# A decoder layer on one core: the last two pairs of the down projection interleaved, their joining done through accumulating transfers, and the final norm written into the plan

## The chip, the cores and the metric

One Trainium2 chip, one core. The metric is the device time of one launch in microseconds. Engines are named as in the profile: PE (TensorE matmul) and PEld (its weight loads), DVE (VectorE), ACT (ScalarE), POOL (GpSimd), SP (SyncE, which here only issues transfers).

## The reference, cut to what matters

One layer of a hybrid decoder for 512 prompt rows and 8 sample rows. Attention, gated linear attention and the projections before them are not touched. What matters is the end of the layer and the final norm:

```python
h = x + mix @ w_o
f = jnp.square(jax.nn.relu(rmsnorm(h, g_norm2) @ w_up))
x = h + f @ w_down            # D_MODEL = 1024, D_FF = 4096
...
y_prompt = rmsnorm(xp, g_final)
y_sample = rmsnorm(xs, g_final)
```

## The kernel before

All rows stand together as 520 columns, 1024 features as 8 tiles (k = 0 to 7) of 128 partitions. The columns are cut into two halves of 260: `one` and `two`. Products are float32 in three passes: a weight is split into a high part (`h`, on ACT) and the rest (`l`, on DVE), and every 128x128 tile is multiplied as high x high, high x low, low x high.

`w_up` and `w_down` are done in 32 *pairs* (units 0 to 31), in four rounds `qd`: four up pairs, then four down pairs for k = 0, 2, 4, 6. A pair makes two feature tiles in both column halves with seven products instead of eight (P1 to P7, each 4x3 = 12 matmuls), from sums and differences of the weights and columns. A unit has three banks in PSUM: `e` takes P5 and then P3, `a` takes P2 (added to a copy of P1, the job `ca`), `x` takes P1, P6, P7, P4 one upon another. The second column half of both tiles is complete after P7 (k5 and k6 save what the banks held in between; `f2` and `t2` add it). P2 and P4 only serve the first half.

The order of all instructions is written out in `PLAN`, one line for each unit. A token is a product (`P1`), a weight's job (`h7`, `l7`, and `s1 s2` for sums of weights) or a job of the unit, with `+` or `-` in front for the next or the previous unit. `pair_mm` goes through a line and issues each token; `turn` and `behind` hold ACT, DVE and PE to that order. DVE steps are issued at L165 (`add`) and L168 (`stt`), ACT steps at L162 (`act`), matmuls of pairs at L259, loads on SP at L121, the weight sums on POOL at L149.

The result `dd` collects the down pairs (`u1` to `u6`) over the first three rounds. In the last round, for tiles k and k+1: `r0 r1` (`settle`, L1488 for its transfer) multiply `dd` by `rv` (the norm's factor, squared, since relu squared is scaled by it afterwards) and add the residual `Hd` from DRAM with an accumulating transfer of POOL. `q` squares for the final norm (ACT), `w` adds the square to `tot` (DVE), `n` multiplies by the final norm's gain (ACT). For k = 4 the residual is not accumulated: `X` loads it with SP, `a0 a1` add it. For k = 6 the last partial sums are multiplied by `rv` before they are added: `m`, `y`, `q`, `w` with the letters `f` (tile 6, half two), `t` (tile 7, half two), `a` (tile 6, half one).

Behind the plan stands the end, in plain code from L1577 on: products of `tot` with ones for both halves (L1583); `rate` (Ln, a DVE step at L1593, Exp, square); the last quarter of `dd` (tile 7, half one) in two pieces of 130 columns, with its own product with ones; `root` (two DVE steps); and `put` (L1605, outputs at L1607), four pieces for half two and five for half one.

The last two lines of the plan before (units 30 and 31):

```
h7 -u5 l5 -r0 P1 h2 -u6 l6 l2 P5 ca l7 h4 -r1 --q1 P6 u1 --q0 l4 --n0 +s1 +h1 P3 u2 +s2 +l1 P7 +h6 --w1 -q0 u4 P2 u3 +h5 -w0 +l5 P4
h4 -u5 h3 l4 -r0 P1 h2 l6 -a0 P5 ca -u6 h7 l3 --n0 -r1 P6 k5 l2 --q1 l7 P3 k6 -a1 ---n1 --w1 -q0 P7 -q1 f2 -w0 --n1 mf P2 t2 yf mt qf -w1 P4 yt w0 qt nt w1 -n1 ma ya qa -n0 wa nf
```

Of the kernel before, what the change touches and what calls it, by code (L numbers as in the profile page):

```python
# [18 lines left out]
D = 1024  # L19
# [19 lines left out]
h7 l5 -x1 --u4 -u5 l6 P1 h2 l7 h3 l3 P5 ca -y0 +s1 P6 u1 -y1 h4 +h5 l4 P3 +X u2 +s2 -u6 l2 P7 +h6 x0 P2 u3 +h1 y0 +l1 P4
h7 l5 -x1 --u4 -y1 P1 l6 l7 P5 ca h3 h2 l3 P6 u1 +s1 h4 +s2 P3 u2 -u4 +h1 l2 l4 P7 +h6 +h3 P2 u3 +h5 +l6 -u6 x0 +l1 P4  # L40
h7 l5 -x1 l7 -u5 P1 -u4 -u6 -y0 h2 l3 --u5 P5 ca +s1 h4 -y1 P6 k5 l4 +h1 l2 +l1 P3 k6 +s2 P7 f2 +h6 +h3 P2 t2 +h5 +l3 rt2 rf2 +l6 P4
-sf2 l5 -st2 h7 -rf1 l7 P1 -ht2 h2 -c0 +s1 -sf1 -rt1 -c1 P5 ca -c3 -st1 +s2 -hT0 h4 l2 P6 k5 -lT0 +h1 -c2 -ht1 -lt2 -hT2 P3 k6 +l1 -hf1 -lT2 -hT1 -lt1 -lf1 P7 +h6 -lT1 l4 +h3 P2 t2 +h5 f2 rt2 +l5 st2 P4
-rf2 l3 -ht2 -sf2 l6 -rf1 -c0 -sf1 P1 +s1 h7 -c3 h2 l7 P5 ca +s2 -hf1 -rt1 l2 h4 P6 k5 -lt2 -c1 -st1 l4 -hT0 -hT1 -lT0 P3 k6 -c2 -ht1 -lf1 -hT2 -lt1 P7 f2 +h6 -lT2 +h1 -lT1 rf2 P2 t2 +h3 +l1 +h5 +l6 rt2 P4
-sf2 l3 -st2 -rf1 l5 h7 P1 -c0 -sf1 -rt1 +s1 -hf1 l7 h4 P5 ca l4 -st1 -ht2 -c1 -ht1 -c3 P6 k5 -lt1 -lt2 h2 -lf1 +h5 -c2 P3 k6 l2 -hT1 +s2 -hT2 -hT0 P7 -lT2 +h6 f2 -lT1 rf2 sf2 -lT0 P2 t2 +h1 +l5 rt2 st2 +l1 P4
-rf1 -sf1 -hf1 -c0 -c3 -lf1 P1 -hT0 -c1 -lT0 h3 -hT1 l6 P5 ca l3 -lT1 h2 h7 P6 u1 -ht2 -lt2 h4 l7 -rt1 P3 u2 -st1 +h1 -c2 l4 -hT2 -ht1 P7 l2 -lt1 -lT2 P2 u3 +s1 +l1 P4
h5 -u4 h6 l5 h7 s2 P1 l6 h3 l7 P5 ca -u5 h2 l3 h4 P6 u1 +h1 +s1 P3 u2 l4 l2 P7 +l1 u4 P2 u3 +h5 -u6 +h6 +s2 P4 Z
l6 h3 l5 h7 -u5 P1 l3 -u6 -z P5 ca +s1 h2 l7 h4 P6 u1 l4 l2 P3 u2 +s2 z0 P7 +h6 +h5 +l6 +h3 P2 u3 +h1 +l1 P4
h7 l5 -u4 -u5 P1 l3 l7 -z1 P5 ca h4 -u6 P6 u1 h2 +s1 +h1 P3 u2 l2 l4 P7 +s2 +l1 P2 u3 +h5 z0 +h6 +h3 P4
l6 l3 l5 P1 h7 -z1 h2 l7 P5 ca h4 l4 P6 k5 +s1 +h1 -u6 -u4 P3 k6 +s2 +l1 l2 P7 +h6 f2 +h3 +l6 rf2 P2 t2 +h5 rt2 +l5 sf2 P4
-st2 --u5 -rf1 l3 -ht2 -sf1 -c0 h7 P1 -c1 -rt1 -lt2 h2 -c3 +s1 P5 ca +s2 -hT0 -hT1 l2 P6 k5 l7 -st1 h4 -c2 -ht1 P3 k6 l4 -hT2 -lT1 +h1 -lT2 -hf1 P7 f2 +h6 -lT0 rf2 -lt1 +h3 -lf1 P2 t2 +h5 +l6 sf2 rt2 +l1 P4  # L50
-st2 l3 -rf1 -sf1 l5 -ht2 P1 h7 -c0 +s1 h2 -c3 -rt1 -c1 P5 ca l2 -st1 h4 l7 -ht1 P6 k5 l4 -hT1 +s2 -hT0 -lt2 -hf1 P3 k6 -lt1 -c2 +h1 -lT0 -lT1 P7 +h6 f2 -lf1 -hT2 +h3 -lT2 P2 t2 rf2 +h5 +l6 rt2 +l1 sf2 P4
h7 l5 -st2 l3 -rf1 -ht2 P1 -c0 -sf1 +s1 -rt1 -st1 -c3 -hf1 -c1 P5 ca l7 h4 +s2 h2 P6 k5 -lf1 l2 -hT1 -c2 -hT0 l4 -ht1 P3 k6 -lt2 +h5 -lT0 -hT2 -lt1 P7 f2 +h6 -lT2 rf2 -lT1 sf2 P2 t2 +h1 +l5 rt2 st2 +l1 P4
-rf1 -sf1 -hf1 l6 -c0 -lf1 h3 P1 -c3 -rt1 -hT0 -c1 -lT0 -hT1 P5 ca l3 -lT1 -st1 -ht1 P6 u1 h7 -ht2 l7 -lt2 h4 h2 P3 u2 -c2 l2 -hT2 +h1 P7 -lt1 l4 -lT2 P2 u3 +s1 +l1 +h6 P4
s2 h5 l5 P1 h7 h2 l7 l6 P5 ca h3 -u5 h4 l3 P6 u1 l2 P3 u2 +s1 l4 P7 +h6 +h1 P2 u3 +h7 -u6 +l1 P4
# [27 lines left out]
class Build:  # L82
# [155 lines left out]

    def pair_mm(self, plan):


        nc, i = self.nc, self.cur
        self.cur += 1
        acts, banks, jobs = self.units[i]
        self.load_sums(i)
        if i + 2 < len(self.panels):
            self.load_panel(i + 2)
        e = banks["e"] = self.pm.tile([P, 2, 512], F32, tag="m", name="mps")[:, 0, :HC]
        a, x = banks["a"], banks["x"] = [self.bank("mps")[:, :HC] for _ in range(2)]
        into = {"P5": e, "P3": e, "P2": a}  # L250
        for t in plan.split():
            n = t.lstrip("+-")
            if n[0] == "P":
                p, ks = n.split(".") if "." in n else (n, "0123")
                hi, lo = self.ready[i][p]
                for k in map(int, ks):
                    xh, xl = acts(p, k)
                    for y, (w, u) in enumerate(((hi, xh), (hi, xl), (lo, xh))):
                        mm = nc.tensor.matmul(into.get(p, x), w[:, k], u, start=(p in ("P1", "P5") and k == 0 and y == 0),  # L259
                                              stop=(k == 3 and y == 2), skip_group_check=True)  # L260
                        self.behind(mm, self.last)
                        self.last = mm
            else:
                j = i + t.count("+") - t.count("-")
                job = self.units[j][2] if j in self.units else {}
                job[n]() if n in job else self.weight(j, n)
# [963 lines left out]
    def run(self):  # L1230
# [159 lines left out]
        with pool("late") as p:  # L1390
# [70 lines left out]
            def extras(qd, k, b):  # L1461
# [23 lines left out]
                def settle(x):  # L1485
                    self.add(dd[:, k + x], dd[:, k + x], rv, op=ALU.mult)
                    if k != 4:
                        nc.gpsimd.dma_start(dd[:, k + x], Hd[:, k + x], accum_op=ALU.add)  # L1488
# [96 lines left out]
            def turn(m):  # L1585
                return self.turn("DVE", m)
# [195 lines left out]
```

## Time and profile before

| | |
|---|---|
| median of 3 runs | 872.91 us (872.46 to 873.63) |
| profiled execution | 870.76 us, of it the span 869.0 us |
| PE, DVE, ACT, POOL busy | 98%, 78%, 57%, 13% of the span |
| granted TensorE clock, mean | 0.994 |
| transfers | 187 MB, 216 GB/s in the mean |

Times in the profile count from the first instruction of the span. "Busy" is the union of an engine's instructions; matmuls are pipelined, so the recorded 0.28 us of one overlap, and a new one starts every 0.12 us. Idle time is shown with the engine that ended it.

### The profile page before, as it was taken

The numbers are of one execution on the slowest core, as the hardware profiler recorded it, in microseconds if no ns is written. First come the engines' busy times: TensorE is split into PE (matmuls) and PEld (weight loads), VectorE is DVE, ScalarE is ACT, GpSimd is POOL, SyncE is SP. The second block draws the span as 40 slices with busy tenths as digits, with TensorE's granted clock in tenths as the row PEclk, the third lists the DMA queues.
The fourth block names the chain that finished last, engine by engine and source line by source line (L and its number), as shares of the span: only waits on it lengthen the run. The fifth ranks groups of instructions, "written<-read, shape, count | busy, mean of one in ns | idle before, by whom it ended". The sixth has DMA issues, their size and how long they took to land.

```text
span 869.0 us, 19702 instructions
## 1 busy us (share of the span) xinstructions
PE 854.3 (98%) x7768; PEld 835.7 (96%) x7768; DVE 677.6 (78%) x1423; ACT 491.7 (57%) x1081; POOL 109.5 (13%) x149
## 2 busy tenths in 40 slices
PE   9999999999999999999999999999999999999993
PEld 9999999999999999999999999999999999999993
DVE  6867576766765958767656578988999899889997
ACT  7233423453644645345733456986895489459764
POOL 1111000001111111003000121111111111111020
PEclk9999999999999999999999999999999999999997
DMA  7478576554767466536599896787686667687662
GB/s 264 127 270 275 207 278 236 208 202 152 264 231 277 169 241 227 190 124 240 184 353 346 317 323 199 177 244 206 181 224 171 171 175 188 172 208 205 179 115 98
DMA packets 56149, 187.31 MB, mean 216 GB/s; under 512 B 7852, under 2 KB 12596, under 8 KB 53080
## 3 DMA queue, kind: packets, MB, share of 16 engines
q1 hardware_dynamic: 41224, 131.10, 42.9%
q0 software_dynamic: 14544, 54.54, 24.5%
q8 instruction: 61, 1.00, 0.4%
q10 hardware_dynamic: 288, 0.40, 0.1%
q14 instruction: 32, 0.26, 0.1%
HBM read 170.16 MB, written 56.30 MB: 261 GB/s over the span
## 4 chain that ended last, share of the span: by engine, by line
PE 92%; DVE 3%; ACT 2%; DMA 1%; issue 1%; POOL 0%; DVEq 0%; ACTq 0%
PE mps L301 48%; PE mps L259 33%; PE lev L896 1%; PE mps L467 1%; DMA dd<-Hd 1%; PE sps L642 1%; PE pvp L675 1%; DVE dd L165 1%; DVE wlo L165 1%; PE gpu L1009 1%; PE gpo L1005 1%; PE ptp L659 1%; PE vps L606 1%; PE gpo L1007 1%; PE gso L1077 1%
## 5 line engine op out<-in xcount | busy, mean ns | idle before, releaser
L301 PE MATMUL mps<-uh,wlo 128*128 128x260 f32 x896 | 255.9, 286 | 0.0
L301 PE MATMUL mps<-uh,whi 128*128 128x260 f32 x896 | 255.7, 285 | 0.0
L301 PE MATMUL mps<-ul,whi 128*128 128x260 f32 x896 | 255.5, 285 | 0.0
L162 ACT ACTIVATE whi<-raw 128x512 fp32r<-128x512 f32 (+1 forms) x218 | 134.2, 619 | 183.2 <-PE mps L301 142.3
L165 DVE TENSOR_TENSOR wlo<-raw,whi 128x512 fp32r<-128x512 f32 (+1 forms) x218 | 148.2, 684 | 50.6 <-ACT whi L162 46.9
L301 PEld LDWEIGHTS mps<-uh,wlo 128*128 128x128 f32 x896 | 168.7, 188 | 2.5 <-issue 1.7
L301 PEld LDWEIGHTS mps<-ul,whi 128*128 128x128 f32 x896 | 168.7, 188 | 1.1 <-issue 0.3
L301 PEld LDWEIGHTS mps<-uh,whi 128*128 128x128 f32 x896 | 168.7, 188 | 0.8 <-issue 0.3
L259 PE MATMUL mps<-fh,whi 128*128 128x260 f32 x256 | 72.5, 283 | 0.0
L259 PE MATMUL mps<-hl,whi 128*128 128x260 f32 x256 | 72.3, 282 | 0.0
L259 PE MATMUL mps<-Tl,whi 128*128 128x260 f32 x256 | 72.2, 282 | 0.0
L259 PE MATMUL mps<-hh,wlo 128*128 128x260 f32 x256 | 72.2, 282 | 0.0
L259 PE MATMUL mps<-Th,whi 128*128 128x260 f32 x256 | 72.2, 282 | 0.0
L259 PE MATMUL mps<-Th,wlo 128*128 128x260 f32 x256 | 72.2, 282 | 0.0
L259 PE MATMUL mps<-fh,wlo 128*128 128x260 f32 x256 | 72.1, 282 | 0.0
L259 PE MATMUL mps<-hh,whi 128*128 128x260 f32 x256 | 72.1, 282 | 0.0
L259 PE MATMUL mps<-fl,whi 128*128 128x260 f32 x256 | 71.9, 281 | 0.0
L162 ACT ACTIVATE whi<-s 128x512 fp32r<-128x512 f32 x64 | 39.0, 624 | 25.4 <-PE mps L259 10.9
L162 ACT ACTIVATE whi<-sums 128x512 fp32r<-128x512 f32 x64 | 39.9, 626 | 16.1 <-PE mps L259 15.7
L259 PEld LDWEIGHTS mps<-Tl,whi 128*128 128x128 f32 x256 | 48.1, 188 | 0.2 <-DVE Tl L165 0.2
L259 PEld LDWEIGHTS mps<-fh,whi 128*128 128x128 f32 x256 | 48.2, 188 | 0.1
L259 PEld LDWEIGHTS mps<-fl,whi 128*128 128x128 f32 x256 | 48.2, 188 | 0.0
(369 smaller groups left out, 2105.9 us busy)
## 6 DMA issues: line engine op xcount, KB each, us to landing
raw<-in_w_in SPq DMA_DIRECT2D x55, 512.0 KB, 3.7
out_ca3v<-in_ca3v SPq DMA_DIRECT2D x64, 256.0 KB, 4.1
out_ca3k<-in_ca3k SPq DMA_DIRECT2D x32, 256.0 KB, 4.2
sums<-in_w_up SPq DMA_DIRECT2D x16, 512.0 KB, 5.8
sums<-in_w_up POOLq DMA_DIRECT2D x16, 512.0 KB, 6.1
raw<-in_w_up SPq DMA_DIRECT2D x16, 512.0 KB, 5.2
sums<-in_w_down SPq DMA_DIRECT2D x16, 512.0 KB, 3.8
raw<-in_w_down SPq DMA_DIRECT2D x16, 512.0 KB, 5.0
```

Source lines behind the costliest of these rows:

```text
L162: return self.turn("ACT", self.nc.scalar.activation(*args, **kw))
L165: return self.turn("DVE", self.nc.vector.tensor_tensor(out, a, b, op=op))
L259: mm = nc.tensor.matmul(into.get(p, x), w[:, k], u, start=(p in ("P1", "P5") and k == 0 and y == 0), stop=(k == 3 and y == 2), skip_group_ ...
L301: mm = self.nc.tensor.matmul(o[:, :HC], wt, x[:, k, j * HC:(j + 1) * HC], start=(k == 0 and n == 0), stop=(k == kt - 1 and n == 2))
L467: self.last = nc.tensor.matmul(ps[i][:, j, :HC], wt, u[:, k, j * HC:(j + 1) * HC], start=(k == 0 and n == 0), stop=(k == KT - 1 and n == 1))
L606: nc.tensor.transpose(pt[:, r * P:(r + 1) * P], vt[:, r * P:(r + 1) * P], self.c["ident"])
L642: m = nc.tensor.matmul(pss[hh][:, hp, c], Q[rows, i, b * P:(b + 1) * P], K[rows, i, ks], start=True, stop=True)
L659: nc.tensor.transpose(pt[:, hh, x], prs[hp][:, hh, x * P:(x + 1) * P], self.c["ident"])
L675: m = nc.tensor.matmul(po[64 * hh:64 * hh + 64, hp * P:(hp + 1) * P], v, pTs[hp][:, hh, x], start=(x == first), stop=(x == 1))
L896: m = self.nc.tensor.matmul(out, w, x, start=True, stop=True)
L1005: nc.tensor.matmul(po[:, :256], ST[:, c], V[:, c], start=True, stop=(c == 0))
L1007: nc.tensor.matmul(po[:, :256], qe[:, c * P:(c + 1) * P], st, start=False, stop=True)
```

## The change

1. `pair_mm` is split: `product` issues the products of any unit, so that a line can hold products of the previous unit too. The last two lines of the plan are now interleaved: unit 30 stops after P7; unit 31 does P1, P5, P6, P3, P7; then follow `-P2 -P4` (unit 30) and `P2 P4` (unit 31).
2. The scaling and joining in parts that k = 6 had is made a function, `closing`, and k = 4 uses it too, in all four quarters (`b` is tile k+1, half one). So `dd` for k = 4 is settled beforehand from three rounds, its residual comes by accumulating transfers, and `X`, `a0`, `a1` are gone. `f` and `t`, and `a` and `b`, share a work tile.
3. The end's steps become tokens (`ending`): `O2 O1` products of `tot` with ones, `Sa` the same of unit 31's `a` squares (which `wa` added to `tot` before), `S0 S1` of the last quarter; `L V X Q` on ACT (`V`, mean and epsilon, was a DVE step and is now `Identity` on ACT), `A R` on DVE, `g d h..x` for the last quarter, `M` the outputs (in half one in the order 0, 2, 4, 1, 3), `no` the gain of the last quarter.
4. All lines of the plan are ordered anew, with the same jobs but for those named here.

The last three lines of the new plan, and the core of the diff:

```
h7 l3 l5 P1 l7 h2 -u4 l2 P5 ca +s1 +h1 -u5 -u6 P6 u1 h4 +l1 +s2 P3 u2 +r1 l4 P7 +h6 -r1 +l6 P2 u3 +h5 -r0 +h3 +l5 P4
h7 l3 +r1 P1 +s1 -u4 -u6 -u5 P5 ca -r1 -r0 P6 k5 +r0 +h5 l7 +h1 +s2 P3 k6 +l5 --q0 +h7 +l1 P7
h6 -f2 l7 ---q1 l6 h3 P1 -t2 -h4 ---w1 ---n0 -mf P5 ca l3 --q1 -l4 -mt P6 k5 -yf --q0 -h2 --w0 P3 k6 -l2 -qf h2 --w1 ---n1 P7 f2 -wf -yt mf -qt -P2 t2 yf mt qf -wt -P4 yt wf qt -ma wt h4 nt l2 O2 --n0 -ya P2 l4 -qa L2 -mb X2 -wa V2 -yb P4 Q2 ma -qb A2 ya -wb -nt qa g0 g1 O1 nf d0 d1 h0x R2 Sa h1x --n1 M23 S0 M20 -nf S1 M21 L1 X1 M22 V1 Q1 no A1 R1 M10 M12 M14 M11 M13
```

```diff
 def settle(x):
     self.add(dd[:, k + x], dd[:, k + x], rv, op=ALU.mult)
-    if k != 4:
-        nc.gpsimd.dma_start(dd[:, k + x], Hd[:, k + x], accum_op=ALU.add)
+    nc.gpsimd.dma_start(dd[:, k + x], Hd[:, k + x], accum_op=ALU.add)
...
-jobs = {"X": load}
+jobs = {}
 for x in range(2):
     jobs[f"r{x}"] = lambda x=x: settle(x)
-    jobs[f"a{x}"] = lambda x=x: self.add(dd[:, k + x], dd[:, k + x], v[x])
-    if k < 6:
+    if k < 4:
         jobs[f"q{x}"] = lambda x=x: final(x)
...
+return jobs if k < 4 else {**jobs, **closing(k, b, gain)}
...
+    for n, x, cc, op in (("f", 0, two, ALU.add), ("t", 1, two, ALU.subtract), ("a", 0, one, ALU.add),
+                         ("b", 1, one, ALU.subtract)):
+        d = dd[:, k + x, cc]
+        src = (lambda n=n: b["a" if n == "a" else "x"]) if cc == one else (lambda n=n: s[n])
+        jobs["m" + n] = lambda n=n, cc=cc, src=src: self.add(place(n), src(), rv[:, cc], op=ALU.mult)
+        jobs["y" + n] = lambda n=n, d=d, op=op: self.add(d, d, s[n], op=op)
+        jobs["q" + n] = lambda n=n, d=d: self.act(s[n], d, AF.Square)
+        jobs["w" + n] = lambda n=n, cc=cc: self.add(tot[0][:, cc], tot[0][:, cc], s[n])
...
+def ending(b, s, gain):
...
+    jobs = {"O2": lambda: ones("2", tot[0][:, two], start=True, stop=True),
+            "O1": lambda: ones("1", tot[0][:, one], start=True), "Sa": lambda: ones("1", s["a"]),
+            "no": lambda: gain(1, one)}
...
+        jobs["V" + n] = lambda n=n: self.act(w(n, 1), v[n], AF.Identity, scale=1 / D, bias=self.eps)
...
 for plan in PLAN.strip().split("\n"):
     self.pair_mm(plan)
-self.pace(1000)
...
+assert not self.copies
```

More of the change, by code (lines that the diff above doesn't have):

```diff
@@ L39 @@
[L39 to L42, printed above, removed]
@@ L237, in start_panels, with product @@
         self.at = np.cumsum([0.0] + [10.04 if p[1] == PAIR else 5.74 for p in panels])
+    def product(self, i, p, ks):
+        acts, b, _ = self.units[i]
+        hi, lo = self.ready[i][p]
+        for k in map(int, ks):
+            xh, xl = acts(p, k)
+            for y, (w, u) in enumerate(((hi, xh), (hi, xl), (lo, xh))):
+                mm = self.nc.tensor.matmul({"P5": b["e"], "P3": b["e"], "P2": b["a"]}.get(p, b["x"]), w[:, k], u,
+                                           start=(p in ("P1", "P5") and k == 0 and y == 0),
+                                           stop=(k == 3 and y == 2), skip_group_check=True)
+                self.behind(mm, self.last)
+                self.last = mm
     def pair_mm(self, plan):
-        nc, i = self.nc, self.cur
+        i = self.cur
         self.cur += 1
-        acts, banks, jobs = self.units[i]
+        banks = self.units[i][1]
         self.load_sums(i)
@@ L247, in pair_mm @@
             self.load_panel(i + 2)
-        e = banks["e"] = self.pm.tile([P, 2, 512], F32, tag="m", name="mps")[:, 0, :HC]
-        a, x = banks["a"], banks["x"] = [self.bank("mps")[:, :HC] for _ in range(2)]
-        into = {"P5": e, "P3": e, "P2": a}
+        banks["e"] = self.pm.tile([P, 2, 512], F32, tag="m", name="mps")[:, 0, :HC]
+        banks["a"], banks["x"] = [self.bank("mps")[:, :HC] for _ in range(2)]
         for t in plan.split():
             n = t.lstrip("+-")
+            j = i + t.count("+") - t.count("-")
             if n[0] == "P":
[L254 to L262, printed above, removed]
+                self.product(j, *n.split(".")) if "." in n else self.product(j, n, "0123")
             else:
-                j = i + t.count("+") - t.count("-")
                 job = self.units[j][2] if j in self.units else {}
@@ new lines, in ending, with ones, w, g @@
+            def ending(b, s, gain):
+                v = {}
+                def ones(n, i, cc=one, start=False, stop=False):
+                    if n not in v:
+                        v[n] = self.bank("r3")[:, :HC]
+                    mm = nc.tensor.matmul(v[n][:, cc], self.ones, i, start=start, stop=stop)
+                    self.behind(mm, self.last)
+                    self.last = mm
+                def w(n, x):
+                    if ("w", n) not in v:
+                        v["w", n] = self.late.tile([P, KT, P], F32, tag="sums", name="sums", bufs=3)
+                    return v["w", n].rearrange("p k n -> p (k n)")[:, x * HC:(x + 1) * HC]
+                def g(x, cc):
+                    if "g" not in v:
+                        v["g"] = work()
+                    return v["g"][:, x * HC + cc.start:x * HC + cc.stop]
+                def out(n, cc, y, z):
+                    c = slice(KT * cc.start + y * HC, KT * cc.start + z * HC)
+                    self.turn("DVE", nc.vector.tensor_tensor(
+                        ya[:, c].rearrange("p (k c) -> p k c", k=z - y), dd[:, y:z, cc],
+                        w(n, 2).unsqueeze(1).to_broadcast([P, z - y, HC]), op=ALU.mult))
+                    (nc.scalar if n == "1" and y % 3 == 1 else nc.sync).dma_start(O["yT"][:, c], ya[:, c])
+                ya = self.big("yt").rearrange("p a b -> p (a b)")
+                jobs = {"O2": lambda: ones("2", tot[0][:, two], start=True, stop=True),
+                        "O1": lambda: ones("1", tot[0][:, one], start=True), "Sa": lambda: ones("1", s["a"]),
+                        "no": lambda: gain(1, one)}
+                for y in range(2):
+                    bb = slice(y * HC // 2, (y + 1) * HC // 2)
+                    d = dd[:, KT - 1, bb]
+                    jobs[f"g{y}"] = lambda bb=bb: self.add(g(0, bb), b["x"][:, bb], rv[:, bb], op=ALU.mult)
+                    jobs[f"d{y}"] = lambda bb=bb, d=d: self.add(d, d, g(0, bb), op=ALU.subtract)
+                    jobs[f"h{y}x"] = lambda bb=bb, d=d: self.act(g(1, bb), d, AF.Square)
+                    jobs[f"S{y}"] = lambda bb=bb, y=y: ones("1", g(1, bb), bb, stop=y == 1)
+                for n, cc, parts in (("2", two, (0, 1, 4, 7, 8)), ("1", one, (0, 1, 3, 5, 7, 8))):
+                    jobs["L" + n] = lambda n=n: self.act(w(n, 0), v[n], AF.Ln, scale=1 / D, bias=self.eps)
+                    jobs["V" + n] = lambda n=n: self.act(w(n, 1), v[n], AF.Identity, scale=1 / D, bias=self.eps)
+                    jobs["X" + n] = lambda n=n: self.act(w(n, 2), w(n, 0), AF.Exp, scale=-0.5)
+                    jobs["Q" + n] = lambda n=n: self.act(w(n, 0), w(n, 2), AF.Square)
+                    jobs["A" + n] = lambda n=n: self.stt(w(n, 0), w(n, 0), -0.5, w(n, 1), op0=ALU.mult, op1=ALU.mult)
+                    jobs["R" + n] = lambda n=n: self.stt(w(n, 2), w(n, 0), 1.5, w(n, 2), op0=ALU.add, op1=ALU.mult)
+                    for x, (y, z) in enumerate(zip(parts, parts[1:])):
+                        jobs[f"M{n}{x}"] = lambda n=n, cc=cc, y=y, z=z: out(n, cc, y, z)
@@ L1576, in run @@
                 self.pair_mm(plan)
-            self.pace(1000)
-            one, two = slice(0, HC), slice(HC, NT)
-            x, k = self.units[self.cur - 1][1]["x"], KT - 1
-            pr = {}
-            def mm(o, i, start, stop):
-                self.behind(nc.tensor.matmul(o, self.ones, i, start=start, stop=stop), self.last)
-            def turn(m):
-                return self.turn("DVE", m)
-            def rate(n, cc):
-                r = {z: work()[:, :HC] for z in "avr"}
-                pr[n, "w"] = r
-                self.act(r["a"], pr[n], AF.Ln, scale=1 / D, bias=self.eps)
-                turn(nc.vector.tensor_scalar(r["v"], pr[n], 1 / D, EPS, op0=ALU.mult, op1=ALU.add))
-                self.act(r["r"], r["a"], AF.Exp, scale=-0.5)
-                self.act(r["a"], r["r"], AF.Square)
@@ L1609, in run @@
-            ya = self.big("yt").rearrange("p a b -> p (a b)")
-            pr["two"], pr["one"] = (self.bank("r3")[:, :HC] for _ in range(2))
-            total = tot[0]
-            mm(pr["two"], total[:, two], True, True)
-            mm(pr["one"], total[:, one], True, False)
-            g, sq = (work()[:, :HC] for _ in range(2))
-            rate("two", two)
-            for y in range(2):
-                bb = slice(y * HC // 2, (y + 1) * HC // 2)
-                self.add(g[:, bb], x[:, bb], rv[:, bb], op=ALU.mult)
-                self.add(dd[:, k, bb], dd[:, k, bb], g[:, bb], op=ALU.subtract)
-                self.act(sq[:, bb], dd[:, k, bb], AF.Square)
-                mm(pr["one"][:, bb], sq[:, bb], False, y == 1)
@@ L1622, in run @@
-            root("two")
-            put("two", two, 0, 1)
-            put("two", two, 1, 4)
-            self.act(dd[:, k, one], dd[:, k, one], AF.Copy, scale=self.g("fin", k))
-            rate("one", one)
-            put("two", two, 4, 7)
-            root("one")
-            put("two", two, 7, 8)
-            for y, z in ((0, 1), (1, 3), (3, 5), (5, 7), (7, 8)):
-                put("one", one, y, z)
+            assert not self.copies
 def _offsets():
```

118 lines of the change are left out of this document (48 added, 70 removed).

## The prediction

> **What bounds the kernel now.** I read the page first, then the table of stages, then TensorE's waits, then the timeline of the last 20 us. TensorE (PE) is busy for 98% of the span.
>
> ```profile
> span 869.0 us, 19702 instructions
> PE 854.3 (98%) x7768; PEld 835.7 (96%) x7768; DVE 677.6 (78%) x1423; ACT 491.7 (57%) x1081; POOL 109.5 (13%) x149
> ```
>
> Stages (us, then busy time of PE, PEld, DVE, ACT, POOL, the granted clock, DMA share, GB/s), and whom PE waited for from 530 us on:
>
> ```profile
> 530.00:671.00 141.00, 141.00 (x1179) 140.82 (x1178) 126.62 (x251) 114.45 (x267) 16.16 (x14) 1.00 0.71 194
> 672.00:853.00 181.00, 181.00 (x1513) 180.91 (x1513) 167.65 (x335) 125.45 (x281) 24.41 (x22) 1.00 0.67 170
> 853.00:869.00 16.00, 2.68 (x11) 1.27 (x9) 9.95 (x23) 6.51 (x15) 0.00 (x0) 0.69 0.36 134
> ```
> ```profile
> PE r L1583 <- ACT t L162: 1.8, 1, 1.8
> PE r L1583 <- DVE tr L165: 1.3, 2, 1.0
> ```
>
> Through all 32 pairs (530 to 853 us) PE has no gap at full clock, and DVE is busy for 91% ((126.62+167.65)/322). PE's only waits are in the last stage. So the change can gain only behind the last product, and can lose wherever PE comes to wait. The tail, from the timeline (start, duration, engine, line, operation; in brackets the idle time before it):
>
> ```profile
> 847.27 0.28 PE L259 MATMUL mps<-FT,wlo 128*128 128x260 f32 x1
> ...
> 847.58 0.39 ACT L162 ACTIVATE P<-mps 128x260 f32<-128x260 f32 x1 [0.53 <-PE mps L259]
> ...
> 850.57 0.42 DVE L165 TENSOR_TENSOR t<-mps,P 128x260 f32<-128x260 f32 x1
> ...
> 850.90 0.42 DVE L165 TENSOR_TENSOR dd<-dd,t 128x260 f32<-128x260 f32 x1
> ...
> 852.89 0.28 PE L259 MATMUL mps<-fl,whi 128*128 128x260 f32 x1
> 853.01 0.28 PE L259 MATMUL mps<-fh,wlo 128*128 128x260 f32 x1
> ...
> 854.68 1.33 ACT L162 ACTIVATE dd<-dd,gcols 128x520 f32<-128x520 f32 x2
> 854.81 0.43 DVE L165 TENSOR_TENSOR tr<-tr,t 128x260 f32<-128x260 f32 x1 [0.48 <-ACT t L162]
> ...
> 855.92 0.46 ACT L162 ACTIVATE t<-r,eps 128x260 f32<-128x260 f32 x1
> 856.41 0.87 ACT L162 ACTIVATE t<-t 128x260 f32<-128x260 f32 x2
> 856.41 0.43 DVE L1593 TENSOR_SCALAR t<-r 128x260 f32<-128x260 f32 x1 [1.17 <-ACT t L162]
> 856.76 0.28 DVE L165 TENSOR_TENSOR t<-mps,acc 128x130 f32<-128x130 f32 x1
> 857.07 0.29 DVE L165 TENSOR_TENSOR dd<-dd,t 128x130 f32<-128x130 f32 x1
> 857.28 0.28 DVE L165 TENSOR_TENSOR t<-mps,acc 128x130 f32<-128x130 f32 x1
> 857.40 0.31 ACT L162 ACTIVATE t<-dd 128x130 f32<-128x130 f32 x1
> ...
> 860.30 0.96 DVE L1605 TENSOR_TENSOR yt<-dd,t 128x780 f32<-128x780 f32 x1
> 861.18 0.88 DVE L168 SCALAR_TENSOR_TENSOR t<-t 128x260 f32<-128x260 f32 x2
> 861.98 2.93 DVE L1605 TENSOR_TENSOR yt<-dd,t 128x260 f32<-128x260 f32 x6
> 863.38 1.90 ACTq L1607 DMA_DIRECT2D out_yT<-yt  x2
> ```
>
> The last product starts at 853.01, yet the step that needs it (the 128x130 `t<-mps,acc`) only at 856.76: DVE first works for the second column half and twice stands idle for ACT (0.48 and 1.17). The last output is issued at 863.38+1.90-0.34 = 864.94 (an issue on that queue takes 0.34). An output takes 2.3 us to land, the rest to 869.0 is the program's end:
>
> ```profile
> DMA to landing us min/median/max: 2.3/2.3/2.3
> ```
>
> **The sum.** I laid the queues of PE, DVE and ACT side by side in the plan's order, each instruction starting when its engine is free and its inputs are there, with durations from these rows. On DVE one 128x260 step follows the last after 0.34 (850.57 to 850.90), one of 130 columns after 0.21, one of 780 after 0.88 (860.30 to 861.18), one of 520 after 0.61 (2.93 = 2x0.34 + 3x0.61 + 0.42). On ACT a scaling of 520 columns takes 0.62 behind another (1.33-0.71), a dependent step 0.45. A matmul takes 0.12 (852.89 to 853.01), and its bank can be read 0.31 after its last start (847.27 to 847.58). A split's second half takes 0.60:
>
> ```profile
> 844.09 0.68 DVE L165 TENSOR_TENSOR wlo<-s,whi 128x512 fp32r<-128x512 f32 x1
> 844.69 0.69 DVE L165 TENSOR_TENSOR dd<-dd,t 128x520 f32<-128x520 f32 x1
> ```
>
> The same laying out of the plan before, from line 25 on, puts its last issue at 864.82, 0.12 short of the trace, with no gap on PE until the end. That is its error.
>
> *Removed work.* Unit 30 loses the two `X` loads (SP), two 520-wide adds `a0 a1`, six sums from the banks and two 520-wide `w`: on DVE 2x0.61 + 6x0.34 + 2x0.61 = 4.5. *Added:* `f2 t2` and four each of `m`, `y`, `w`, 14x0.34 = 4.8 on DVE, and on ACT two copies (0.39 each by the row at 847.58) and four half squares for two whole ones, under 1 us more. Both `V` steps move from DVE to ACT (0.4 each), and `wa` of unit 31 becomes a product with ones (`Sa`). So the work stays about equal; what counts is where it lies.
>
> *The new order.* `-P2 -P4` of unit 30 and `P2 P4` of unit 31 are now the last 48 matmuls, 48x0.12 = 5.75. So unit 31's P7 starts its last at 853.01-5.75 = 847.26. To this come 0.1 where line 28's P1 waits for the late `-lf1`, and 0.31 until it can be read: `t2` starts at 847.67.
> - DVE: `t2 yf mt -wt yt wf -ma wt`, 8x0.34: 850.39, the last done 0.08 later. -P2 and -P4 end on PE at 847.36+25x0.12 = 850.36, so `O2` (which needs `wt`) starts at about 850.55: PE idles 0.2.
> - `O2`: a 260-column product with ones amid dense work takes two passes of 0.22 (671.38 to 672.06 below, with three steps of 0.22 between four passes): 0.44. Then P2 and P4: their last starts at 850.99+23x0.12 = 853.75, 0.74 later than before. This is the change's cost.
>
> ```profile
> 671.38 1.04 PE L1476 MATMUL r<-acc,ones 128*128 128x260 f32 x4
> 672.06 0.48 PE L259 MATMUL mps<-fh,whi 128*128 128x260 f32 x1
> ```
>
> - DVE goes on: `l2` 0.60, `-ya` 0.34, `l4` 0.60, `-mb -wa -yb ma` 4x0.34, to 853.29; 0.15 wait for ACT's `Q2`; `A2 ya -wb` 3x0.34, to 854.46. PE's last bank is readable at 854.06, so DVE decides. `g0 g1 d0 d1` 4x0.21: 855.30.
> - ACT: `h0x` at 855.22, `h1x` 0.22 behind it (an estimate; 0.31 at most, the duration of the row at 857.40) to 855.75, then `--n1` and `-nf` 2x0.62, `L1` at 856.90, `X1 V1 Q1` to 858.52 (0.49+0.33+0.37+0.42). DVE has `R2 M23 M20 M21 M22` meanwhile (0.46+2x0.34+2x0.88 = 2.9) to 858.2: both end nearly together.
> - `A1` 858.55, `R1` 859.01, `M10` 859.47, then 0.34+0.61+0.34+0.61: `M13` from 861.36 to 862.05. Last issue 862.08.
>
> Against 864.82 that is 2.74 earlier: 3.5 won behind the last product, 0.74 given back. The last transfer is now 260 KB on SP instead of 130 KB on ACT; SP's outputs of that size land in the same 2.3. The profiled execution, 870.76 (span 869.0), would become 868.0 (span 866.3). It lies 2.15 under the median, so the median goes from 872.91 to 870.2.
>
> *The accumulating transfers.* POOL now issues eight instead of six for `dd` (k=4 joins), seven between 828.8 and 839. Their price in a queue, before:
>
> ```profile
> 825.36 1.19 POOL L149 DMA_DIRECT2D sums<-in_w_down  x1 [9.13 <-DVE wlo L165]
> 826.08 3.19 POOL L1488 DMA_DIRECT2D dd<-Hd  x3
> 833.62 0.86 POOL L1488 DMA_DIRECT2D dd<-Hd  x1 [4.35 <-DVE dd L165]
> 836.37 0.86 POOL L1488 DMA_DIRECT2D dd<-Hd  x1 [1.89 <-DVE dd L165]
> ```
> ```profile
> 827.88 9.05 DMA dd<-Hd
> ```
> ```profile
> DMA to landing us min/median/max: 4.2/6.7/9.1
> ```
>
> One alone lands after 4.2. The bunch of one 512 KB and three 260 KB took from 825.36 to 836.93; less 4.2 for the first 260 KB, the other 1032 KB took 7.4, or 1.9 for each 260 KB. At the widest, all 11.6 shared by four transfers, it is 2.9. I take 1.9, since the sizes are known and the queue moved all four without a pause. Then unit 29's two (`-r1 -r0` on DVE at 834.9 and 835.5) land near 840.5 and 842.5; `--q1` and `--q0` on ACT want them at 842.3 and 843.7. Behind them on ACT wait `k5`, `-h2` and `k6`, without which PE can't enter P3 and P7; `k6` has 0.8 to spare. The removed `X` loads ran on SP long before their use, with nothing behind them there until 830: nothing gained.
>
> ```profile
> 821.38 0.99 SPq L121 DMA_DIRECT2D t<-Hd  x2
> 830.38 0.33 SPq L121 DMA_DIRECT2D rb<-in_w_down  x1
> ```
>
> **Rivals.**
> 1. *The accumulating transfers come late (slower).* At 2.9 each they land at 845.8 and 848.7. ACT stands still in front of `k5` and `k6`, PE waits 1.1, 1.1 and 2.0 at unit 31's P6, P3 and P7 and 0.6 more at `O2`: last issue 866.9, 2.1 after the old one, 875.0. The point from which nothing is gained is 2.55 each; under 2.15 all is hidden. For: landings of 9.05. Against: that one stood behind 1032 KB.
> 2. *The packed tail doesn't pack.* From 847 to 862 DVE has hardly a gap in my lists. If waits like the 0.48 and 1.17 of before come back at other places, 1.65 is lost: gain 1.1, 871.8. Against: the same method is 0.12 off on a tail with many hand-overs.
> 3. *PE waits somewhere earlier.* Lines 1 to 29 of the plan are reordered too, with DVE at 91%. One gap of 1 to 2 us gives 871.2 to 872.2. My lists show only the 0.1 at line 28.
> 4. *`Identity` needs another table.* `V1` would then bring one load in front of it and one in front of `L1` behind `V2`: 2x1.28 by the row below, 870.2+2.6 = 872.8. Against: after the last load (L1382, at 433 us) copies, squares, Relu, Ln and Exp all run without another.
>
> ```profile
> L1382 ACT ACT_TABLE_LOAD x1 | 1.3, 1283 | 0.0
> ```
>
> On this the Trainium skill ("ScalarE: Activation LUTs", "Table sets: the hidden batching unit") says that cheap functions, identity among them, are in every set; by that rule rival 4 falls away and the sum stays 870.2. Its section "What ACT_TABLE_LOAD costs" gives 1283 ns for a load, as the row does, and 2.66 us with the drain; by that figure two switches would give an estimate of 875.5. No run so far shows `Identity` itself.
>
> **Chances.** Forecast (gain 2 to 3.5, so 869.4 to 870.9): 0.66. Rival 1: 0.05 at its full price, 0.05 in part (871 to 873). Rival 2: 0.13. Rival 3: 0.08, half of it under 871.2. Rival 4: 0.03. A measurement here can tell 0.2%, 1.75 us: faster is under 871.16. Faster 0.66 + 0.04 + 0.02 (the mild end of rivals 1 and 2) = 0.72; slower (over 874.66) 0.05; the same 0.23. The range 869.3 to 872.4 holds the forecast, rival 2, rival 3 and the milder part of rival 1, and leaves out about 0.15.
>
> **What would show it.** Right: PE without a gap until `O2`; the last product's start at about 853.7 in the profile; the 128x130 `t<-mps,acc` within 1 us of it (3.75 before); the last DVE step near 861.4; span near 866.3. Wrong: PE waits for `mps` at L162 between 843 and 848 with ACT waiting for `dd<-Hd` (rival 1); a table load behind 850 us (rival 4); a PE gap between 540 and 840 (rival 3); DVE idle over 1 us behind 854 (rival 2).

## The result, and the profile after

| | before | after |
|---|---|---|
| median | 873.01 us (872.46 to 873.63) | 868.17 us (867.97 to 869.03) |
| ratio, 95% interval | | 0.9945 [0.9932, 0.9958] |
| profiled execution, its span | 870.76 us, 869.0 us | 868.2 us, 866.4 us |

The changed kernel is 4.84 us faster, with an interval of 3.7 to 5.9 us. The forecast was 2.7 us faster, 870.2 us; its range ended at 869.3. So the sign was right and the size was not. The same two kernels measured twice more gave 0.9958 [0.9946, 0.9971] and 0.9958 [0.9945, 0.997], 3.7 and 4.1 us, so what is to be explained is about 4 us; the first comparison shows the upper end of it.

The page's first lines, and whom PE waited for from 530 us on:

```profile
span 866.4 us, 19720 instructions
PE 854.6 (99%) x7770; PEld 836.0 (96%) x7770; DVE 676.0 (78%) x1424; ACT 490.9 (57%) x1087; POOL 115.4 (13%) x151
```
```profile
PE r L1564 <- DVE tr L165: 0.5, 1, 0.5
```

PE's busy time is what it was (854.6 for 854.3), in a shorter span. Of the waits of before behind the products (one of 1.8 for ACT, two of together 1.3 for DVE) one of 0.5 is left. The stages, with the same columns as in the prediction (busy time of PE, PEld, DVE, ACT, POOL, clock, DMA share, GB/s):

```profile
530.00:671.00 141.00, 141.00 (x1180) 140.82 (x1179) 125.42 (x249) 113.49 (x266) 16.16 (x14) 1.00 0.70 192
672.00:853.00 181.00, 180.99 (x1508) 180.60 (x1507) 168.75 (x341) 125.44 (x286) 26.09 (x24) 1.00 0.68 173
```

All the reordered lines up to `O2` at 851 us run without a gap on PE. The end, from the timeline (start, duration, engine, line, operation; "x2" is a run of two):

```profile
851.13 0.28 PE L246 MATMUL mps<-fh,wlo 128*128 128x260 f32 x1
...
851.42 0.71 PE L1564 MATMUL r<-tr,ones 128*128 128x260 f32 x2
...
852.67 0.46 ACT L162 ACTIVATE sums<-r,eps 128x260 f32<-128x260 f32 x1
...
853.49 0.46 ACT L162 ACTIVATE sums<-r,eps 128x260 f32<-128x260 f32 x1
...
854.30 0.43 DVE L168 SCALAR_TENSOR_TENSOR sums<-sums 128x260 f32<-128x260 f32 x1
...
854.73 0.28 PE L246 MATMUL mps<-fh,wlo 128*128 128x260 f32 x1
...
855.32 0.49 DVE L165 TENSOR_TENSOR t<-mps,acc 128x130 f32<-128x130 f32 x2
855.46 0.71 PE L1564 MATMUL r<-tr,ones 128*128 128x260 f32 x2 [0.46 <-DVE tr L165]
...
857.95 0.46 ACT L162 ACTIVATE sums<-r,eps 128x260 f32<-128x260 f32 x1
...
859.57 0.89 DVE L168 SCALAR_TENSOR_TENSOR sums<-sums 128x260 f32<-128x260 f32 x2 [0.26 <-ACT sums L162]
860.50 2.60 DVE L1580 TENSOR_TENSOR yt<-dd,sums 128x260 f32<-128x260 f32 x5
```
```profile
860.96 2.50 SPq L1583 DMA_DIRECT2D out_yT<-yt  x3
```

`O2` starts at 851.42, 0.29 behind the matmul ahead of it, so PE idles 0.17 there (a matmul takes 0.12). The last product starts at 854.73, and the 128x130 step that needs it only 0.59 later, not 3.75 as before. From 854.30 on DVE has one idle stretch, 0.26. The last output is issued at 860.96 + 2.50 - 0.33 = 863.13 (an issue on SP takes 0.33); from there to the end of the span are 3.29 us, where the kernel before had 868.96 - 864.94 = 4.02.

Two profiles can be compared only after the part ahead of the pairs, which the change leaves alone, has been taken off. The first and the last start of one kind of pair product, before and after:

```profile
L259 PE MATMUL mps<-hh,whi x256: 277/282/285, 530.5 to 845.6; 128*128 128x260 f32 x128
```
```profile
L246 PE MATMUL mps<-hh,whi x256: 278/282/286, 531.5 to 843.7; 128*128 128x260 f32 x128
```

The pairs of after begin 1.0 us later. Matmul for matmul, after is 1.00 to 1.04 behind before from the 150th (22 us) to the 5,100th: between these two profiles the shift arises in the first 22 us and stays. There their chains of waits differ: before, the first run of products starts at 7.45, after it starts at 8.43, right behind one transfer. From the profile after:

```profile
1.65 5.11 DMA xr<-in_xT
6.77 0.02 issue
6.79 0.02 ACTq L449
6.80 0.05 issue
6.86 0.74 ACT uh L449
7.59 0.02 issue
7.62 0.77 DVE ul L451
8.39 0.04 issue
8.43 0.63 PE mps L471 x3
```

The change touches nothing there. So each profile is cut in three below: up to the first product of the pairs, from there to the last issued output, and from that to the end of the span. All values are read from the traces in hundredths.

| profile | start | pairs to last issue | behind it | span |
|---|---|---|---|---|
| before | 530.48 | 334.46 | 4.02 | 868.96 |
| after | 531.51 | 331.62 | 3.29 | 866.42 |
| after less before | +1.03 | -2.84 | -0.73 | -2.54 |

The lists of the prediction gave -2.74 for the middle column, 0 for the last, and took the base as it stood.

### The profile page after: what moved, and what is told of

Read it like the earlier page. It is cut to its first block, busy times and chain, and to the rows that moved or that the text cites. A ratio compares the mean times of both kernels' runs of the same rounds, so it can differ in the third digit from the quotient of the medians.

```text
span 866.4 us, 19720 instructions
## 1 busy us (share of the span) xinstructions
PE 854.6 (99%) x7770; PEld 836.0 (96%) x7770; DVE 676.0 (78%) x1424; ACT 490.9 (57%) x1087; POOL 115.4 (13%) x151
## 4 chain that ended last, share of the span: by engine, by line
PE 95%; ACT 2%; DVE 1%; DMA 1%; issue 0%; SPq 0%; DVEq 0%; ACTq 0%
PE mps L305 48%; PE mps L246 36%; PE lev L900 1%; PE mps L471 1%; PE sps L646 1%; PE pvp L679 1%; PE gpu L1013 1%; PE gpo L1009 1%; PE ptp L663 1%; PE vps L610 1%; PE gpo L1011 1%; DMA xr<-in_xT 1%; PE gso L1081 1%; ACT dd L162 1%; ACT sums L162 0%
## 5 line engine op out<-in xcount | busy, mean ns | idle before, releaser
L246 PEld LDWEIGHTS mps<-Th,wlo 128*128 128x128 f32 x256 | 48.2, 188 | 0.0
L246 PEld LDWEIGHTS mps<-hh,wlo 128*128 128x128 f32 x256 | 48.2, 188 | 0.0
```

The source lines that it names most:

```text
L246: mm = self.nc.tensor.matmul({"P5": b["e"], "P3": b["e"], "P2": b["a"]}.get(p, b["x"]), w[:, k], u, start=(p in ("P1", "P5") and k == 0 an ...
```

## The experiments

The questions: what are the parts of the 2.84 (theory: the interleaving; rival: the joining of k = 4, or the end's steps alone); did the accumulating transfers cost the kernel before time in executions other than the profiled one (theory B of e1 and e5; theory A is that only the start varies), so that removing that gave the rest; and what shortens the time behind the last issue.

**The kernel before again (e1), and three more single executions of it with their profiles (e9, e10, e11).** No edit.

> The kernel before, unchanged. Its timed executions lay at 873.0 us, its profiled one at 870.76, and the change was measured at 868.17 where I had subtracted 2.74 from the wrong or the right base. Theory A (the start): the 2.1 us between the profiled and the timed executions of before lie in the first 25 us, where PE waits for the first loads, and have nothing to do with the change. Then, whatever this run's time, the stretch from the first pair's matmul to the last issued output is 334.3 us as in the first profile, and a span above 869.0 shows as a later start of the pairs. Theory B (the pairs): in most executions of before PE waits some 2 us within the pairs or the end, and the rewritten plan took that wait away. Then a run of 873 has a stretch of about 336.4 us with a gap on PE or a later tail.

> The kernel before, a third profile, to see which of three stretches varies from one execution to the next: until the first pair's matmul (530.5 and 533.3 us in the two profiles so far; 531.0 to 532.2 in those of all variants), from there to the last issued output (334.5 and 335.3, the second with a PE gap of 0.8 in line 31), and behind it (4.0 in both). A: the first stretch holds most of the spread, and its usual value is near 531.6. B: the second does, with PE gaps behind ACT's wait for dd<-Hd.

> The same, a fourth profile of the kernel before: A: pairs and end 334.5 us, the time set by the start. B: pairs and end 335 us or more, with a PE gap.

> The same, a fifth profile of the kernel before: A: pairs and end 334.5 us, the time set by the start. B: pairs and end 335 us or more, with a PE gap.

Measured: e1 872.03 us, ratio 1.0005 [0.9996, 1.0014] (the execution that was profiled took 874.44); the single executions 872.5, 872.19 and 871.83 us. The parts of their profiles:

| profile | start | pairs to last issue | behind it | span |
|---|---|---|---|---|
| before | 530.48 | 334.46 | 4.02 | 868.96 |
| e1 | 533.34 | 335.30 | 4.02 | 872.66 |
| e9 | 532.45 | 334.28 | 4.01 | 870.73 |
| e10 | 532.06 | 334.29 | 4.07 | 870.42 |
| e11 | 531.42 | 334.63 | 4.00 | 870.05 |

The profile that the prediction was built on has the earliest start of the five, 1.5 us under their mean (531.95), and no other of them comes to the pairs before 531.4. It was a short execution: its 870.76 us lie below the lowest of the runs shown beside it (872.46), and of the 64 executions of the same kernel in the later comparisons three are as short. Their medians are 871.98, 871.95 and 872.37.

The start does not vary in the first 25 us alone, as theory A had it. e1 comes to the pairs 2.86 later than before: 0.93 of this arises in the first 22 us, 0.69 at 305 us and 0.99 at 456 us (on the axis of before), where PE stands still for ACT and for DVE. Its waits there, of which the profile of before has none:

```profile
PE mps L301 <- DVE gB L1404: 0.8, 1, 0.8
PE gsp L1094 <- ACT ov L1089: 0.6, 1, 0.6
```

Within the pairs, a late accumulating transfer reaches PE in e1 alone. Whom PE and ACT waited for there, and the landing of that line's transfers:

```profile
PE mps L259 <- ACT whi L162: 0.7, 1, 0.7
```
```profile
ACT t L162 <- DMA dd<-Hd: 2.3, 1, 2.3
```
```profile
DMA to landing us min/median/max: 4.0/6.8/9.9
```

ACT stands 2.3 us before a square whose input isn't there yet, and PE waits 0.7 for what stands behind it on ACT. In the profile of before the same wait of ACT was 1.5 and cost nothing:

```profile
ACT t L162 <- DMA dd<-Hd: 1.5, 1, 1.5
```

**The squares that wait for the transfers, later (e5, e12).** In line 30 of the kernel before, `--q1 --q0 --n0` move behind `+h6`, so that nothing urgent stands behind the waiting square:

```diff
-... h4 -r1 --q1 P6 u1 --q0 l4 --n0 +s1 +h1 P3 u2 +s2 +l1 P7 +h6 --w1 -q0 u4 ...
+... h4 -r1 P6 u1 l4 +s1 +h1 P3 u2 +s2 +l1 P7 +h6 --q1 --q0 --n0 u4 --w1 -q0 ...
```

> The kernel before with one move: in line 30 the three ACT steps that wait for accumulating transfers of unit 28 (--q1, --q0, --n0) stand behind +h6, some 3 us later; nothing else. In the second profile of before ACT waited 2.30 us there for a transfer (1.48 in the first) and PE then 0.7 us for a weight; in the first PE did not wait. Laid side by side, before loses nothing up to 0.8 us of lateness of these transfers and then one for one, this variant nothing up to 2 us. Theory B (late transfers cost before up to 2 us in most executions, and the new plan took that away): this variant is 0.5 to 2 us faster than before, and its profile shows no PE gap in the pairs. Theory A (the start): as before within 0.3 us.

> The variant of before with the three ACT steps of line 30 moved behind +h6, a second profile. It was not faster than before (ratio 1.0008). If the waits for the transfers had only been moved to another place, its pairs and end show a PE gap at line 31 and more than 334.9 us; if such waits are rare, 334.9 us again without a gap, and its times are set by the start like those of before.

Measured: 872.94 us, ratio 1.0008 [0.9995, 1.0021]; the single execution of e12 took 871.89 us. ACT's wait for `dd<-Hd` is gone from both profiles, PE has no gap within the pairs, and the time is not shorter. The edit itself costs a little: the middle parts are 334.89 and 334.90, 0.4 more than before's, so it could hide a gain of that size, but not one of 2 us. With no such PE wait in four of the five profiles above, theory B falls for these runs: late transfers explain e1's 0.8 us, not a gain in most executions. For the executions of the first comparison it is not decided, since the only profile from there is the short one.

**The changed kernel again (e2, e15).** No edit.

> The changed kernel, unchanged, on the same chip. A: about 868.2 us again if its start is settled by its program, else anywhere between 866 and 870.5; the stretch from the first pair's matmul to the last issued output 331.5 us in any case. B: 868.2 us and 331.5 us.

> The changed kernel once more, unedited. If its gain is what the profiles' parts give (2.84 up to the last issue and 0.65 behind it), it is 3.5 us faster, ratio 0.9960. If the first comparison was typical, 4.8 us, ratio 0.9945. The start up to the first pair lies between 530.5 and 533.4 either way.

Measured: 868.32 us, ratio 0.9958 [0.9946, 0.9971], and 868.3 us, 0.9958 [0.9945, 0.997]. From the first pair to the last issue their profiles take 331.60 and 331.62, behind it 3.51 and 3.36, with starts of 532.24 and 531.42. The changed kernel's own times repeat within 0.15 us (868.17, 868.32, 868.3); it is the kernel before that stood at 873.01, then 871.98 and 872.37.

**The order of the products undone (e3, e7).** The changed kernel with unit 30 finished before unit 31 begins; all jobs stay. e7:

```diff
-h7 l3 +r1 P1 +s1 -u4 ... P3 k6 +l5 --q0 +h7 +l1 P7
-h6 -f2 l7 ---q1 ... P7 f2 -wf -yt mf -qt -P2 t2 yf mt qf -wt -P4 yt wf ... O2 --n0 -ya P2 l4 ... P4 Q2 ma ...
+h7 l3 +r1 P1 +s1 h2 -u4 ... P7 +h6 f2 +l6 P2 t2 +h5 +l5 P4
+h7 h3 ---q1 -mf ... P7 f2 -nt mf -nf P2 t2 yf mt --w0 qf yt wf qt wt nt --n0 P4 O2 ma ya L2 ...
```

e3 is the same with `nt` moved behind the output of tile 7, half two, so that this output leaves out its gain.

> The changed kernel with the products of the last two units in the old order (unit 30 ends with its own P2 and P4), the weights' jobs and the steps around them put where that order needs them; k=4's accumulating transfers and the end's tokens stay. By the queues laid side by side: last product at 853.3 on the time axis of the first profile, last issue 863.7, against 862.1 with the interleaving and 864.8 before: 1.6 us slower than the changed kernel, 869.8 us. If the interleaving did nothing and the rest is all from the other parts: 868.2 us.

> The changed kernel with the products of the last two units in the old order and the steps around them arranged for it; accumulating transfers and the end's tokens stay. Laid side by side its last issue is at 863.7 on the axis of the first profile, against 862.1 for the changed kernel: 1.6 us slower, 869.9 us. If the interleaving were worth nothing: 868.3 us; if it were the whole gain: 871 us or more.

Measured: e3 870.79 us, ratio 0.9981 [0.9972, 0.999], 1.0 above what was expected; e7 870.33 us, 0.9982 [0.9973, 0.9991], 2.0 above the changed kernel (expected 1.6). e7's middle part is 333.29, 1.67 above after's 331.62, and PE waits behind the products again:

```profile
PE r L1564 <- ACT t L162: 1.6, 1, 1.6
PE r L1564 <- DVE tr L165: 0.8, 1, 0.8
```

e7's order of the steps differs too, so this is one number for both: the order of the products and of the steps that it lets go on beside them carries 1.7 of the 2.84 us.

**The residual of k = 4 loaded and added, as before (e4).**

```diff
-    nc.gpsimd.dma_start(dd[:, k + x], Hd[:, k + x], accum_op=ALU.add)
+    if k != 4:
+        nc.gpsimd.dma_start(dd[:, k + x], Hd[:, k + x], accum_op=ALU.add)
...
-jobs = {}
+jobs = {"X": load}
...
+    jobs[f"a{x}"] = lambda x=x: self.add(dd[:, k + x], dd[:, k + x], v[x])
```

with `+X` in the plan behind unit 29's P3 and `a0`, `a1` on DVE in unit 30.

> The changed kernel with k=4's residual loaded by SP and added by DVE (two adds of 520 columns, X, a0 and a1 in lines 29 and 30) instead of joined by accumulating transfers. By the queues laid side by side DVE's two adds of 0.61 us make O2 0.46 later and all behind it: 868.6 us. If X's loads were what cost before 2 us in its timed executions (theory B, with the loads as the cause): 870 us or more.

Measured: 869.81 us, ratio 0.9974 [0.9965, 0.9983]: 1.5 above e2, and 1.2 above the time expected. The profile splits the miss. The middle part grew by what was expected: 332.09, 0.47 more, and `O2` now waits 0.5 for DVE:

```profile
851.39 0.71 PE L1566 MATMUL r<-tr,ones 128*128 128x260 f32 x2 [0.50 <-DVE tr L165]
```

The rest is behind the last issue: 4.04 as in the kernel before, with the outputs in the order of the changed kernel. Both together give 1.0 (against e2's profile) to 1.2 (against after's) of the 1.5.

**The settling of the last two pairs one product later (e6).** In line 30 `-r1 -r0` move from behind `ca` to behind `+s2`, which puts their transfers about one product later on the queue.

> The changed kernel with one move: in line 30 unit 29's two settles (-r1 -r0), whose transfers --q1 and --q0 wait for, come some 2 us later (behind +s2). That gives it the margin of before: laid side by side 0.8 us of lateness stay free, then one for one. B: 0.3 to 2 us slower than the changed kernel, 868.6 to 870.3 us, with ACT waiting for dd<-Hd and, in a slow execution, PE for ACT at unit 31's P6, P3 or P7. A: 868.3 us, unchanged.

Measured: 869.16 us, ratio 0.9968 [0.9956, 0.998], 0.8 above e2; the two intervals overlap, but the middle part shows the same, 332.34, 0.7 above after's. ACT, which waited for no `dd<-Hd` in the profile after, does so here, and PE's wait at `O2` becomes 0.6:

```profile
ACT t L162 <- DMA dd<-Hd: 0.8, 1, 0.8
ACT tr L162 <- DMA dd<-Hd: 0.6, 1, 0.6
```
```profile
PE r L1564 <- DVE tr L165: 0.6, 1, 0.6
```

The mechanism of rival 1 exists; in the changed kernel the transfers are issued just early enough for it not to work.

**More sums on PE (e8).** `-wa` and `-wb`, which add unit 30's squares to `tot` on DVE, become products with ones (`Ta`, `Tb`) behind the last product, and two gains move into gaps of ACT:

```diff
-... wf -yt mf -qt -P2 t2 yf mt qf -wt -P4 yt ... O2 --n0 -ya P2 ... X2 -wa V2 ... A2 ya -wb -nt ... d1 h0x R2 Sa h1x --n1 M23 ...
+... wf -yt mf -qt --n1 -P2 t2 yf mt qf -wt -P4 --n0 yt ... O2 -ya P2 ... X2 V2 ... A2 ya -nt ... d1 Ta h0x R2 Tb Sa h1x M23 ...
```

> The changed kernel with a lighter tail: unit 30's squares of half one go to PE as two more products with ones (Ta, Tb) instead of two DVE adds (-wa, -wb), and the gains --n1 and --n0 fill ACT's gaps between -qt, qf and qt. If DVE's dense queue sets the end, as the prediction's sum has it, the end is 0.6 us earlier (last issue 861.5 against 862.1): 867.7 us. If PE or the transfers set it: no change or slower by the 0.9 us of the two products.

Measured: 867.78 us, ratio 0.9956 [0.9944, 0.9969]; span 865.62, middle part 331.10, so 0.5 less than after, and no wait of PE from 530 us on. The medians differ by the same 0.5 (868.32 for e2), but the two ratios cannot be told apart. By its median and by its profile it is the shortest kernel measured here.

**The order of the outputs, both ways (e13, e14).** In the changed kernel the old order, in the kernel before the new one:

```diff
-... A1 R1 M10 M12 M14 M11 M13
+... A1 R1 M10 M11 M12 M13 M14
```
```diff
-for y, z in ((0, 1), (1, 3), (3, 5), (5, 7), (7, 8)):
+for y, z in ((0, 1), (3, 5), (7, 8), (1, 3), (5, 7)):
```

> The changed kernel with the outputs of half one issued in the old order (tiles 0, 1-2, 3-4, 5-6, 7: the last is 130 KB on ACT's queue) instead of 0, 3-4, 7, 1-2, 5-6 (the last is 260 KB on SP's). Theory A, the order of the outputs sets the 0.6 to 0.7 us behind the last issue: from the last issued output to the end of the span 3.9 to 4.1 instead of 3.3 to 3.5, first pair to last issue as before at 331.6, time 0.6 above the changed kernel: about 868.8. Theory B, something else (fewer transfers or semaphores to be waited for at the end of the program): 3.3 to 3.5 stays, time 868.2.

> The kernel before with the outputs of half one in the new order (0, 3-4, 7, 1-2, 5-6). Theory A, the order: from the last issue to the end of the span 3.3 to 3.5 instead of 4.0, time 0.6 below the kernel before: about 871.4 to 872. Theory B, something else: 4.0 stays, and the time with it. Both: 334.3 to 334.6 from the first pair to the last issue.

Measured: e13 868.3 us, ratio 0.9949 [0.9936, 0.9963], the same median as e15 beside it; e14 871.92 us, 0.9992 [0.9983, 1.0001]. Behind the last issue e13 takes 3.26 and e14 4.12: the 0.7 does not move with the order. Theory A of these two runs, the order, falls.

What do the traces show? Each transfer raises a semaphore, a counter, when it has landed. At the end of the program SP waits for one such semaphore after the other, in a fixed order, and then issues three `DRAIN` instructions. The waits, by the numbers of the semaphores in the traces, with the time at which each was passed; marked is the one that the record of the last output's issue names:

```
               issue   100     102      103     104     105     107     108     109      first drain
before         864.94  866.93  867.31*  867.40  867.47  867.54  867.92  868.00  868.05   868.13
e14_new_order  865.07  866.75  867.55*  867.63  867.71  867.78  868.14  868.22  868.28   868.35
e4_x_load      863.09  864.69  865.40*  865.47  865.52  865.59  865.64  865.74  865.81   866.18
after          863.13  863.62  863.69   863.75  863.81  863.87  864.04  864.78  865.43*  865.50
```

The marked wait is passed 0.43 to 0.56 us after the last packet of the output (865.00 in after, 864.95 in e4, 866.99 in e14). In e14 and e4 it is 102, early in the list, and six waits (0.41 to 0.73 us) are still to be gone through behind it. In before, where the last output is ACT's, it is 102 too, passed 0.43 after the last packet (866.88), with the same six behind it (0.74). In after it is 109, the last in the list, and all others are already behind. SP's drains in the same profiles, before and after:

```profile
L1761 SPq DRAIN  x3: 7/7/7, 868.1 to 868.4; - x3
```
```profile
L1753 SPq DRAIN  x3: 7/7/130, 865.5 to 866.1; - x3
```

The first drain comes 868.1 - 864.9 = 3.2 behind the last issue before, and 865.5 - 863.1 = 2.4 after. e4 (3.1) has the long end and differs from after in the two `X` loads on SP, their two adds, and the two accumulating transfers that these replace. In all, nine profiles with the `X` loads have 3.96 to 4.12 behind the last issue, and eight without them 3.26 to 3.51. That the `X` loads go with the long end is shown. How they do it can be read from the same traces. The issues of SP and ACT take the eight semaphores 100, 102 to 105 and 107 to 109 in turn, in all seventeen profiles without a break. With the `X` loads there are 386 such issues and the last output gets 102; without them there are 384, and it gets 109, two places earlier in the turn. From the last issue to the passing of its own wait all seventeen take 2.30 to 2.51; from there to the first drain the nine take 0.78 to 0.83 and the eight 0.06 to 0.07. So the difference lies in the waits that are still behind that of the last output. No run moved the last output's place by itself, for example with one load more elsewhere. And that the place came out last is chance: nothing in the change aimed at it.

## Why the prediction was right and wrong

**Right: the order laid out on the queues.** With 1.03 taken from the profile after, the steps stand beside their forecasts:

| step | forecast | profile after, less 1.03 |
|---|---|---|
| `O2` starts | 850.55 | 850.39 |
| last product | 853.75 | 853.70 |
| `g0` (first 128x130 step) | 854.46 | 854.29 |
| `L1` | 856.90 | 856.92 |
| `A1` | 858.55 | 858.54 |
| last output's issue | 862.08 | 862.10 |

The cost of the change (the last product later by 0.74) came out at 0.69 from the first product of the pairs on, the gain behind it at 3.53 for 3.5. "PE idles 0.2" at `O2` is 0.17. The sum to the last issue was 2.74; with the error of 0.12 that the lists had on the kernel before, 2.84 was measured. That the last issue agrees to 0.02 is partly luck: `O2` and `g0` came 0.16 and 0.17 earlier than forecast, and from `g0` to `L1` it took 0.19 longer.

**Wrong: "The last transfer is now 260 KB on SP instead of 130 KB on ACT ... land in the same 2.3."** The landing is indeed the same; what was mis-sized is the term behind it, "the rest to 869.0 is the program's end", which was held constant. It is 0.73 shorter in this pair of profiles, and 0.64 in the means (4.02 over the five profiles of before; 3.29, 3.51 and 3.36 for after). It goes with the removed `X` loads, which the prediction priced: "The removed `X` loads ran on SP long before their use ... nothing gained." Nothing was gained where they ran; the gain stands at the program's end. It is the one part of the miss whose cause the runs show: with it and the 0.1 of the lists the forecast would have been 869.4. The other 1.2 stand in the base, below.

**Wrong: "It lies 2.15 under the median, so the median goes from 872.91 to 870.2."** The 2.15 were carried over whole, as if the kernel took 872.91 in the middle. In the later comparisons its median was 871.95 to 872.37. Against these, 1.2 to 1.6 of the 2.15 belong to the profiled execution, whose pairs began 1.5 before the mean of the five profiles, and 0.5 to 1.0 to the median of three runs, which stood too high as a base. Taking the gain from a median was sound; this median was not confirmed. The forecast for the profile itself, 868.0, was 0.2 off, and that is luck: the profile after began its pairs 1.03 later, and its end was 0.73 and its middle 0.10 shorter than forecast, which nearly cancel. The forecast for the median was 2.0 off. A sign stood in the table: 870.76 is below every run beside it.

The account of the 4.74 us from 872.91 to 868.17: 2.84 to the last issue, 0.73 behind it, and 1.17 that these parts don't hold. In the second and third comparison, 3.66 and 4.07, the same parts leave 0.1 and 0.5. The change does not touch the part where the starts scatter, and the means of the starts (531.95 for five profiles of before, 531.72 for after, e2 and e15) differ by less than they scatter. Why the kernel before was 1 us slower at first than in the next comparison stays open. The later comparisons ran on several chips (e1 to e8 on one, e9 to e12 on another, e13 to e15 on a third), and the record does not name that of the first; whether a chip makes the difference was not tried.

**The rivals.** *1, late accumulating transfers:* not in the changed kernel. Their landing from 820 us on, against the 4.2/6.7/9.1 of before:

```profile
DMA to landing us min/median/max: 5.0/6.4/7.3
```

Unit 29's two landed at 841.65 and 843.91, with 1.03 off 840.6 and 842.9, for 840.5 and 842.5; the next landed at 845.19. So one transfer of this bunch landed 2.3 us behind the one ahead of it and the next 1.3, around the 1.9 that the prediction took. e6 shows what one product less of margin costs. *2, the tail does not pack:* DVE's one idle stretch from 854 on is 0.26. *3, a gap earlier:* none in 530 to 851 us in this profile. *4, another table for `Identity`:* the last of the table loads in the profile after is the old one, at 434.2 us, and the `Identity` rows at 853.49 and 858.78 take 0.46 with nothing ahead of them:

```profile
L1386 ACT ACT_TABLE_LOAD  x1: 1283/1283/1283, 434.2 to 434.2; - x1
```

The Trainium skill ("ScalarE: Activation LUTs", "Table sets: the hidden batching unit") says that identity is in every set; this trace, with no load behind 434.2, agrees.

**Which edit gave what.** The interleaving 1.7 (e7), the joining of k = 4 by transfers 0.47 up to the last issue (e4). What is left of the 2.84, about 0.7, falls to the end's steps written into the plan; no run tried these alone, and the parts need not add up.

## What to carry to other kernels

Laying the queues of all engines side by side with durations from the trace forecast each of the six steps compared above to 0.2 us; what failed was the program's end behind them, held constant, and the base that the gain was set against. Before a difference is added to a median, look whether the profiled execution lies inside the range of the runs, cut it at a fixed point (here the first product of the pairs), and see whether its distance from the median arose ahead of that point; and take the median from more than three runs. Count the end of the program as a part of its own: what two transfers removed elsewhere did to the list of waits there was worth 0.7 us, beside 2.84 for all that the lists held.

## What was not expected of the hardware

- The start up to the first pair scatters between 530.48 and 533.34 us over five profiles of one kernel. Part of a shift arises in the first 22 us (1.02 between before and after, which then stays within 0.04 through 5,000 matmuls; 0.93 in e1), the rest where PE comes to wait later (0.69 and 0.99 more in e1).
- With all engines done and the last output landed, the time to the end of the span is 2.1 us (866.88 to 868.96) or 1.4 us (865.00 to 866.42). The shorter one goes with the last transfer's semaphore being last in SP's list, and two issues fewer of 386 put it there.
- Accumulating transfers of 260 KB queued behind one another landed 2.3 and 1.3 us apart in the last bunch of the changed kernel; in the bunch of the kernel before, which one of 512 KB leads, the three of 260 KB landed 1.6, 1.3 and 2.9 us behind the transfer ahead of each.
